# A two-layer hybrid decoder trunk: one near-bias row per head with zeros ahead of it, conditioning rows on VectorE alone, one of four branch scalings on ScalarE

## The chip, the cores and the metric

The kernel runs on one core of one Trainium2 chip. The metric is the device time of one execution in microseconds (us); less is better. The engines go by their profile names: PE is TensorE (matmuls and transposes), DVE is VectorE, ACT is ScalarE, POOL is GpSimd, SP is SyncE, which issues most of the transfers.

## What is computed

Two decoder layers on a sequence of 512 tokens of width 1024, batch 1, in float32. Each layer is a mixer and a SwiGLU feed-forward, both between norms that a conditioning vector c shifts, scales and gates:

```
for layer in range(2):
    shift, scale, gate = split(c @ mod_w[layer, 0] + mod_b[layer, 0], 3)
    h = rms_norm(x, norm_w[layer, 0, 0]) * (1 + scale) + shift
    y = mixer_ab(h) if layer == 0 else mixer_cd(h)
    x = x + gate * rms_norm(y, norm_w[layer, 0, 1])
    shift, scale, gate = split(c @ mod_w[layer, 1] + mod_b[layer, 1], 3)
    h = rms_norm(x, norm_w[layer, 1, 0]) * (1 + scale) + shift
    x = x + gate * rms_norm(swiglu(h), norm_w[layer, 1, 1])

# every softmax mixer, per head and block of 128 queries:
s = q @ k.T * scale + rel_tab[bucket(query - key)]     # masked where key > query
o = softmax(s) @ v
```

mixer_ab is native sparse attention (nsa: a compressed, a selected and a window branch, each times its own gate, 8 heads in 2 groups) beside sliding-window attention (swa). mixer_cd is block-sparse attention (moba) beside stick-breaking attention. The bias rel_tab depends on the distance of query and key alone, and is the same for all distances above some bound. With 512 tokens the selected branch of nsa takes all blocks and the window takes all keys, so both are plain causal attention with a bias, over other keys and values.

## The kernel before, in words

Matmuls of float32 data are made of three passes over operands split in a high and a low half: ACT writes the high half (L209), DVE the rest (L210), PE multiplies three times (L221 to L223). Weights stream through a ring of raw buffers that SP fills.

The program has one stage behind the other. In the profiled execution these are: the first norm and projections (to 75 us); swa attention, the compressed keys and the projections of keys and queries (75 to 162); nsa (162 to 245); the output projection of the mixer (248 to 302); the boundary to the first feed-forward (285 to 320); feed-forward 0 (to 670); the boundary and the projections of layer 1 (to 717); moba beside the value projections (717 to 800); stick-breaking (to 882); the output projection and feed-forward 1 (to 1300).

An **attention unit** is four heads of one group against one block of 128 queries, `qb` 0 to 3, so that it sees nk = 128, 256, 384 or 512 keys. `softmax_unit` (L619) makes, per head, two matmuls of the scores into PSUM (L631, L632), then on DVE a sum with the head's bias that also finds the row's minimum (one `tensor_tensor_reduce`, shown as CUSTOM_DVE_ANT; the minimum is fetched by a DVE_READ_ACCUMULATOR behind it), then the exponential on ACT (L646). `full` (L1011) takes the reciprocal of the sum and multiplies by the gate (L1020, L1022), scales the probabilities (`scale_p`, L680: one DVE instruction for all heads at L689 up to 256 keys; above that one per head, on ACT at L694 for as many heads as ACT_SCALE says, on DVE at L696 for the others), and multiplies by the values (`pv`, L650: transposes on PE at L659, a copy on ACT at L661, matmuls at L665). nsa has 16 such units (2 groups, 4 query blocks, selected and window branch), and the compressed branch is added by L1068 to L1073; its softmax is L1051 to L1062. moba has 8 units; there two of four heads were already scaled on ACT.

The bias is not zero only in the last 256 keys of a row. The **near table** NB (L344) holds a row of 256 zeros and, behind it, 256 biases per head; a head is a two-row view, zeros and its own row. A row with 512 keys is one instruction over this view (L637). A row with 384 keys is two: 128 keys with zeros (L641), then 256 with the biases, which starts from the minimum of the first (L644). A row with 256 or 128 keys is one (L644). The table is made twice: before nsa and before moba.

The **conditioning rows** (`mod_rows`, L352) are the product of c with columns of mod_w: a row of layer 0 is 8 steps over a 128x1024 tile of weights (SP loads it into a raw buffer, L377). A step is one DVE instruction that multiplies by a scalar per partition and adds to the sum (L384), or, for a row whose entry in ROW_DVE is 0, a scaling on ACT (L386) and an addition on POOL (L387). Rows 0 to 2 are stepped along with the query projections (two steps per projection) and the nsa units.

What is issued when is set by the scheduler of the language: each engine's instructions are put in an order by a timeline that it keeps for itself, so that every edit may move instructions near and far; each engine then runs its own list in that order and waits at its head. In nsa the front of a unit (scores to exponential) has priority over the back of the one before.

Of the kernel before, what the change touches and what calls it, by code (L numbers as in the profile page):

```python
# [10 lines left out]
F32 = mybir.dt.float32  # L11
F32R = mybir.dt.float32r
AF = mybir.ActivationFunctionType
ALU = mybir.AluOpType
# [115 lines left out]
class Trunk:  # L130
# [3 lines left out]
    MOD_ROW = 2  # L134
    ACT_SCALE = {"swa": 0, "nsa": 0, "moba": 2}
    AHEAD = {"swa": 0, "nsa": 60, "moba": 0}
    PIN = ("nsa",)
    ROW_DVE = (1, 0, 1)
    BIAS_AT = 4
# [204 lines left out]
    def near_table(self, pool):  # L344

        nb = pool.tile([P, 9, 256], F32, tag="NB", name=self.nm("NB"))
        self.nc.gpsimd.memset(nb[:, 0, :], 0.0)
        self.load_near(nb[:, 1:9, :], 0, 8)
        return [nb[:, 0:h + 2:h + 1, :] for h in range(8)]

# [268 lines left out]
    def softmax_unit(self, qb, heads, K, NB, init=None, far=True):  # L619
# [7 lines left out]
        for i, (q, nb) in enumerate(zip(heads, NB)):  # L627
# [6 lines left out]
            st = 3e38 if init is None else init[:, i:i + 1]  # L634
            two = lambda a: a.rearrange("p (b k) -> p b k", b=2)
            if nk == 512:
                red = nc.vector.tensor_tensor_reduce(two(pt), two(ps), nb[:, 0:2, :], 1.0, st, ALU.add, ALU.min, mx[:, i:i + 1])  # L637
            else:
                fw = max(nk - 256, 0)
                if fw:  # L640
                    nc.vector.tensor_tensor_reduce(pt[:, :fw], ps[:, :fw], nb[:, 0, :fw], 1.0, st,  # L641
                                                   ALU.add, ALU.min, mx[:, 4 + i:5 + i])
                    st = mx[:, 4 + i:5 + i]
                red = nc.vector.tensor_tensor_reduce(pt[:, fw:], ps[:, fw:], nb[:, nb.shape[1] - 1, 256 - (nk - fw):], 1.0,  # L644
                                                     st, ALU.add, ALU.min, mx[:, i:i + 1])
            nc.scalar.activation(pt, pt, AF.Exp, bias=mx[:, i:i + 1], scale=-1.0, accum_out=den[:, i:i + 1])  # L646
# [165 lines left out]
    def start(self):  # L812
# [26 lines left out]
        def feature(j):  # L839
            h = self.t_tmp("h", 2, 512)  # L840
            if j == self.BIAS_AT:
                self.bias_tables()
                self.skew_near(8)
                NBs = self.p_at.tile([P, 8, 256], F32, tag="NBs", name="NBs")
                self.load_near(NBs, 8, 8)
                self.NBs = [NBs[:, h:h + 1, :] for h in range(8)]
            acc = self.t_tmp("acc", 2, 256)
# [248 lines left out]
    def attention_ab(self):  # L1096
# [9 lines left out]
        self.skew_near(0)  # L1106
        self.NBn = self.near_table(self.p_at)
        
# [165 lines left out]
```

## Time and profile before

| what | value |
|---|---|
| median of 3 runs | 1304.86 us (1304.48 to 1305.43) |
| the profiled execution's own time | 1301.82 us |
| its span | 1300.0 us, 16642 instructions |
| granted TensorE clock, mean | 0.99 |
| PE busy | 1249.0 us, 96% |
| DVE busy | 683.3 us, 53% |
| ACT busy | 534.0 us, 41% |
| POOL busy | 92.2 us, 7% |

The shares are means over stages that differ much: in the feed-forwards PE is busy and DVE half idle, while in nsa DVE has hardly a gap. So the table says which engine carries the program as a whole, and the stage that an edit touches has to be read by itself. The profiled execution was 3.0 us under the median of the runs; the times in the trace count from the start of its span.

### The profile page before, as it was taken

How to read it: one execution, taken by the hardware profiler on the slowest of the kernel's cores; microseconds unless marked ns; L12 is line 12 of the kernel's file. 1: busy time of each engine (PE TensorE's matmuls, PEld its weight loads, DVE VectorE, ACT ScalarE, POOL GpSimd, SP SyncE). 2: the span in 40 equal slices, each digit the busy share in tenths (PEclk: the TensorE clock that was granted, in tenths of full speed). 3: DMA queues.
4: the chain of work that ended last, by engine and by line, in shares of the span. 5: the costliest groups of instructions: out<-in, count | busy, mean ns of one | idle time of the engine just before them, and what ended most of it. 6: DMA issues, size and time to landing. Idle time of an engine off the chain costs nothing.

```text
span 1300.0 us, 16642 instructions
## 1 busy us (share of the span) xinstructions
PE 1249.0 (96%) x6452; PEld 1021.2 (79%) x6452; DVE 683.3 (53%) x1158; ACT 534.0 (41%) x1015; POOL 92.2 (7%) x118
## 2 busy tenths in 40 slices
PE   6999999998999999999989999999999999999997
PEld 4887765687888888888879777878888888888885
DVE  6659799569457685342265555554733322224223
ACT  4447677642323223232242676773432222223221
POOL 1210600111000100000011000000000000000000
PEclk9999999998999999999999999999999999999999
DMA  9738602548547873333443113215433333333321
GB/s 382 248 91 259 195 21 95 199 145 338 209 152 264 330 259 98 97 96 97 127 162 103 49 50 86 61 34 210 178 85 104 96 96 96 96 97 96 96 97 65
DMA packets 52014, 183.88 MB, mean 141 GB/s; under 512 B 7185, under 2 KB 7329, under 8 KB 50912
## 3 DMA queue, kind: packets, MB, share of 16 engines
q1 hardware_dynamic: 46784, 171.57, 39.3%
q0 software_dynamic: 4720, 10.91, 3.1%
q8 instruction: 51, 0.84, 0.3%
q10 hardware_dynamic: 432, 0.35, 0.1%
q14 instruction: 27, 0.22, 0.0%
HBM read 170.11 MB, written 11.11 MB: 139 GB/s over the span
## 4 chain that ended last, share of the span: by engine, by line
PE 82%; DVE 8%; ACT 4%; DMA 3%; issue 3%; SPq 0%; POOL 0%; DVEq 0%; POOLq 0%; ACTq 0%
PE gu L222 12%; PE gu L223 12%; PE gu L221 12%; PE yacc L221 8%; PE yacc L223 7%; PE yacc L222 7%; PE mm L221 2%; PE mm L222 2%; PE mm L223 2%; PE oT L665 2%; PE z L1243 2%; PE PT L659 2%; DVE wlo L210 1%; PE S L631 1%; PE pc L221 1%
## 5 line engine op out<-in xcount | busy, mean ns | idle before, releaser
L210 DVE TENSOR_TENSOR wlo<-raw,whi 128x1024 fp32r<-128x1024 f32 (+1 forms) x182 | 218.3, 1205 | 372.1 <-ACT whi L209 371.3
L209 ACT ACTIVATE whi<-raw 128x1024 fp32r<-128x1024 f32 (+1 forms) x182 | 189.2, 1045 | 475.1 <-PE gu L222 274.0
L221 PE MATMUL gu<-act,whi 128*128 128x512 f32 (+1 forms) x768 | 284.7, 373 | 4.1 <-ACT act L495 4.1
L222 PE MATMUL gu<-act,whi 128*128 128x512 f32 (+1 forms) x768 | 286.3, 374 | 0.2 <-DVE act L496 0.2
L223 PE MATMUL gu<-act,wlo 128*128 128x512 f32 (+1 forms) x768 | 286.0, 373 | 0.0
L221 PE MATMUL yacc<-whi,act 128*128 128x512 f32 x480 | 186.4, 391 | 1.2 <-ACT whi L209 1.2
L222 PE MATMUL yacc<-wlo,act 128*128 128x512 f32 x480 | 186.7, 390 | 0.0
L223 PE MATMUL yacc<-whi,act 128*128 128x512 f32 x480 | 186.5, 389 | 0.0
L221 PEld LDWEIGHTS gu<-act,whi 128*128 128x128 f32 x768 | 145.0, 190 | 30.0 <-ACT act L495 5.0
L222 PEld LDWEIGHTS gu<-act,whi 128*128 128x128 f32 x768 | 145.9, 190 | 25.3 <-DVE act L496 0.4
L223 PEld LDWEIGHTS gu<-act,wlo 128*128 128x128 f32 x768 | 145.9, 190 | 24.9
L221 PEld LDWEIGHTS yacc<-whi,act 128*128 128x128 f32 x480 | 90.0, 188 | 21.0 <-ACT whi L209 1.7
L223 PEld LDWEIGHTS yacc<-whi,act 128*128 128x128 f32 x480 | 90.1, 188 | 18.8
L222 PEld LDWEIGHTS yacc<-wlo,act 128*128 128x128 f32 x480 | 90.1, 188 | 18.6
L384 DVE SCALAR_TENSOR_TENSOR macc<-act,col,macc 128x1024 f32<-128x1024 f32 x56 | 71.7, 1282 | 13.7 <-DMA macc<-in_mod_b 12.7
L646 ACT ACTIVATE act<-act,den 128x256 f32<-128x256 f32 (+3 forms) x128 | 68.2, 536 | 12.9 <-DVE den L644 9.5
L462 POOL TENSOR_TENSOR rms<-rms,col 128x1 f32<-128x1 f32 x32 | 25.2, 787 | 676.6 <-DVE rms L461 676.6
L221 PE MATMUL mm<-act,whi 128*128 128x512 f32 x160 | 64.2, 401 | 1.2 <-ACT NBc L338 1.2
L223 PE MATMUL mm<-act,wlo 128*128 128x512 f32 x160 | 63.1, 394 | 0.3 <-DVE wlo L210 0.3
L222 PE MATMUL mm<-act,whi 128*128 128x512 f32 x160 | 63.3, 395 | 0.0
L661 ACT ACTIVATE PT<-PT 128x512 f32<-128x512 f32 x74 | 41.4, 594 | 26.6 <-PE PT L659 26.4
L631 PE MATMUL S<-dup,stk 128*128 128x256 f32 (+3 forms) x128 | 44.2, 359 | 5.2 <-DVE den L644 2.7
(231 smaller groups left out, 1620.6 us busy)
## 6 DMA issues: line engine op xcount, KB each, us to landing
raw<-in_wfi SPq DMA_DIRECT2D x88, 512.0 KB, 3.6
act<-in_mod_w SPq DMA_DIRECT2D x28, 1024.0 KB, 7.2
raw<-in_wfo SPq DMA_DIRECT2D x44, 512.0 KB, 3.5
raw<-in_mod_w SPq DMA_DIRECT2D x24, 512.0 KB, 4.3
raw<-in_wcdf SPq DMA_DIRECT2D x18, 512.0 KB, 3.6
act<-in_mod SPq DMA_DIRECT2D x8, 1024.0 KB, 10.6
sc_x<-bnd SPq DMA_DIRECT2D x12, 512.0 KB, 2.7
bnd<-sc_x SPq DMA_DIRECT2D x12, 512.0 KB, 5.3
```

The lines of the kernel that those rows point to most:

```text
L209: nc.scalar.activation(hi[:, :n], raw[:, :n], AF.Copy)
L210: nc.vector.tensor_sub(lo[:, :n], raw[:, :n], hi[:, :n].bitcast(F32))
L221: nc.tensor.matmul(ps, a[0], b[0], start=start, stop=False)
L222: nc.tensor.matmul(ps, a[0], b[1], start=False, stop=False)
L223: nc.tensor.matmul(ps, a[1], b[0], start=False, stop=stop)
L384: nc.vector.scalar_tensor_tensor(accs[i], src, c, accs[i], op0=ALU.mult, op1=ALU.add)
L631: nc.tensor.matmul(ps, qs, K[:, 0, ks], start=True, stop=False)
L646: nc.scalar.activation(pt, pt, AF.Exp, bias=mx[:, i:i + 1], scale=-1.0, accum_out=den[:, i:i + 1])
L659: tr = nc.tensor.transpose(pp[:, m * P:m * P + P], Pt[:, i, c], self.ident)
L661: nc.scalar.activation(t, pp, AF.Copy)
L665: mm = nc.tensor.matmul(oT[DH * e:DH * e + DH, 0:256], V[:, kb], t[:, 256 * e:256 * e + 256], start=first and kb == lo_kb, stop=last and k ...
L1243: nc.tensor.matmul(z[i][:, a, l2:r], st, sph[k2 // 2][:, k2 % 2, 256 * p + l2:256 * p + r], start=False, stop=(k2 == nb - 1 and p == 1), s ...
```

## The change

Three edits in the program. The near table becomes one row of 512 per head, zeros in columns 0 to 255 and the biases behind them, so that a row of any number of keys is one instruction over the last nk columns; the zeros are written for 8 heads in place of one row, and the nsa table is taken from another pool of memory. Row 1 of the conditioning rows goes from ACT and POOL to DVE, as rows 0 and 2. In nsa the first of four heads of a unit with more than 256 keys is scaled on ACT, the other three on DVE; this holds for both the selected and the window branch, since both go through `scale_p`.

```
-    ACT_SCALE = {"swa": 0, "nsa": 0, "moba": 2}
+    ACT_SCALE = {"swa": 0, "nsa": 1, "moba": 2}
...
-    ROW_DVE = (1, 0, 1)
+    ROW_DVE = (1, 1, 1)
...
     def near_table(self, pool):
-        nb = pool.tile([P, 9, 256], F32, tag="NB", name=self.nm("NB"))
-        self.nc.gpsimd.memset(nb[:, 0, :], 0.0)
-        self.load_near(nb[:, 1:9, :], 0, 8)
-        return [nb[:, 0:h + 2:h + 1, :] for h in range(8)]
+        nb = pool.tile([P, 8, 512], F32, tag="NB", name=self.nm("NB"))
+        self.nc.gpsimd.memset(nb[:, :, 0:256], 0.0)
+        self.load_near(nb[:, :, 256:512], 0, 8)
+        return [nb[:, h, :] for h in range(8)]
...
-            two = lambda a: a.rearrange("p (b k) -> p b k", b=2)
-            if nk == 512:
-                red = nc.vector.tensor_tensor_reduce(two(pt), two(ps), nb[:, 0:2, :], 1.0, st, ALU.add, ALU.min, mx[:, i:i + 1])
-            else:
-                fw = max(nk - 256, 0)
-                if fw:
-                    nc.vector.tensor_tensor_reduce(pt[:, :fw], ps[:, :fw], nb[:, 0, :fw], 1.0, st,
-                                                   ALU.add, ALU.min, mx[:, 4 + i:5 + i])
-                    st = mx[:, 4 + i:5 + i]
-                red = nc.vector.tensor_tensor_reduce(pt[:, fw:], ps[:, fw:], nb[:, nb.shape[1] - 1, 256 - (nk - fw):], 1.0,
-                                                     st, ALU.add, ALU.min, mx[:, i:i + 1])
+            red = nc.vector.tensor_tensor_reduce(pt, ps, nb[:, nb.shape[1] - nk:], 1.0, st, ALU.add, ALU.min, mx[:, i:i + 1])
...
-                self.NBs = [NBs[:, h:h + 1, :] for h in range(8)]
+                self.NBs = [NBs[:, h, :] for h in range(8)]
...
         self.skew_near(0)
-        self.NBn = self.near_table(self.p_at)
+        self.NBn = self.near_table(self.p_tmp)
```

The scheduler then gives every engine another order in several places. Line numbers below are those of each kernel's own text; lines behind the near table's edit stand ten lines earlier in the changed kernel.

First place: DVE, at the end of swa and the first query projections, where rows 0 and 1 of the conditioning meet (macc is a row's sum, raw a weight tile, stk a query pair, act the probabilities). Before:

```order
L384 SCALAR_TENSOR_TENSOR macc_1387<-raw_1514,col,macc_1387 128x1024
L1003 RECIPROCAL fac_1058<-fac_1058 128x4
L1002 TENSOR_TENSOR fac_1085<-fac_1085,den_1037 128x4
L384 SCALAR_TENSOR_TENSOR macc_1387<-raw_1556,col,macc_1387 128x1024
L210 TENSOR_TENSOR wlo_1523<-raw_1520,whi_1522 128x1024
L689 TENSOR_TENSOR act_989<-act_989,fac_1058 128x4x256
L1003 RECIPROCAL fac_1085<-fac_1085 128x4
L250 SCALAR_TENSOR_TENSOR stk_1382<-mm_1357,stk_1382 64x512
L689 TENSOR_TENSOR act_989<-act_989,fac_1085 128x4x256
```

Now:

```order
L384 SCALAR_TENSOR_TENSOR macc_1387<-raw_1514,col,macc_1387 128x1024
L993 RECIPROCAL fac_1058<-fac_1058 128x4
L992 TENSOR_TENSOR fac_1085<-fac_1085,den_1037 128x4
L384 SCALAR_TENSOR_TENSOR macc_1517<-raw_1559,col,macc_1517 128x1024
L384 SCALAR_TENSOR_TENSOR macc_1387<-raw_1556,col,macc_1387 128x1024
L210 TENSOR_TENSOR wlo_1523<-raw_1520,whi_1522 128x1024
L679 TENSOR_TENSOR act_989<-act_989,fac_1058 128x4x256
L993 RECIPROCAL fac_1085<-fac_1085 128x4
L250 SCALAR_TENSOR_TENSOR stk_1382<-mm_1357,stk_1382 64x512
L384 SCALAR_TENSOR_TENSOR macc_1517<-raw_1670,col,macc_1517 128x1024
L679 TENSOR_TENSOR act_989<-act_989,fac_1085 128x4x256
```

The first step of row 1 (macc_1517, raw_1559) stands ahead of the last step of row 0, and its second ahead of the last swa scaling; the other six are spread over the query projections up to the compressed softmax.

Second place: ACT in nsa, group 0, the units with 384 and 512 keys (act with den is the exponential, PT the copy of transposed probabilities, sc the compressed branch). Before:

```order
L646 ACTIVATE act_1824,den_1823<-act_1824,den_1823 128x384 x2
L677 ACTIVATE act_1566<-oT_1703 128x2x128
L646 ACTIVATE act_1824,den_1823<-act_1824,den_1823 128x384 x2
L1056 ACTIVATE sc_1806<-sc_1806 128x512
L646 ACTIVATE act_1893,den_1892<-act_1893,den_1892 128x512 x4
L661 ACTIVATE PT_1870<-PT_1865 128x512
L661 ACTIVATE PT_1877<-PT_1872 128x512
L661 ACTIVATE PT_1884<-PT_1879 128x512
```

Now:

```order
L636 ACTIVATE act_1816,den_1815<-act_1816,den_1815 128x384 x3
L636 ACTIVATE act_1881,den_1880<-act_1881,den_1880 128x512
L667 ACTIVATE act_1566<-oT_1701 128x2x128
L636 ACTIVATE act_1881,den_1880<-act_1881,den_1880 128x512
L684 ACTIVATE act_1729<-act_1729,fac_1837 128x384
L1046 ACTIVATE sc_1798<-sc_1798 128x512
L636 ACTIVATE act_1881,den_1880<-act_1881,den_1880 128x512 x2
L651 ACTIVATE PT_1858<-PT_1853 128x512
L651 ACTIVATE PT_1865<-PT_1860 128x512
L651 ACTIVATE PT_1872<-PT_1867 128x512
```

The scaling of one unit's first head (L684) now stands between the exponentials of the next unit; eight such instructions come in nsa.

Third place: PE at the start of the mixer's output projection (yacc is the sum of one of three blocks of tokens, whi and wlo a weight tile's halves; each row occurs twice in the kernel, for two halves of the columns, and is given once). Before:

```order
L221 MATMUL yacc_2676<-whi_2604,act_1566 128x512
L222 MATMUL yacc_2676<-wlo_2605,act_1566 128x512
L223 MATMUL yacc_2676<-whi_2604,act_1567 128x512
L221 MATMUL yacc_2676<-whi_2610,act_1566 128x512
L221 MATMUL yacc_2741<-whi_2604,act_1566 128x512
L222 MATMUL yacc_2741<-wlo_2605,act_1566 128x512
L223 MATMUL yacc_2741<-whi_2604,act_1567 128x512
```

Now:

```order
L221 MATMUL yacc_2782<-whi_2580,act_1566 128x512
L222 MATMUL yacc_2782<-wlo_2581,act_1566 128x512
L223 MATMUL yacc_2782<-whi_2580,act_1567 128x512
L221 MATMUL yacc_2652<-whi_2586,act_1566 128x512
L221 MATMUL yacc_2717<-whi_2586,act_1566 128x512
L221 MATMUL yacc_2782<-whi_2586,act_1566 128x512
L222 MATMUL yacc_2652<-wlo_2587,act_1566 128x512
```

Before, six matmuls with the first weight tile (whi_2604) stood ahead of the first matmul with the second (whi_2610); now 18 with the first (whi_2580, all three blocks of tokens) stand ahead of the first with the second (whi_2586).

On POOL, the zeros and the load of the near table for moba stood ahead of the copies of the keys for moba (L268), and now stand behind the two of its first key tile. In nsa the table's zeros and load keep their place among POOL's transfers.

## Rows read from the trace of the kernel before

**Rows 1.** The page: engines' busy time and the chain that ended last, by engine.

```profile
PE 1249.0 (96%) x6452; PEld 1021.2 (79%) x6452; DVE 683.3 (53%) x1158; ACT 534.0 (41%) x1015; POOL 92.2 (7%) x118
...
PE 82%; DVE 8%; ACT 4%; DMA 3%; issue 3%; SPq 0%; POOL 0%; DVEq 0%; POOLq 0%; ACTq 0%
```

**Rows 2.** Windows: stretch, its length, busy us (instructions), clock, DMA share, GB/s.

```profile
core 0: us, PE busy (x) PEld busy (x) DVE busy (x) ACT busy (x) POOL busy (x), PEclk, DMA share, GB/s
140.00:150.00 10.00, 9.85 (x62) 7.15 (x61) 2.86 (x5) 8.54 (x12) 9.77 (x5) 1.00 0.52 160
...
172.00:217.00 45.00, 40.98 (x276) 25.99 (x276) 43.62 (x156) 32.70 (x99) 2.71 (x4) 1.00 0.26 76
217.00:245.00 28.00, 27.59 (x192) 16.26 (x191) 21.58 (x70) 22.26 (x53) 3.96 (x6) 1.00 0.17 53
...
717.00:800.00 83.00, 79.91 (x448) 62.77 (x447) 42.89 (x126) 57.98 (x130) 1.06 (x2) 1.00 0.19 58
```

**Rows 3.** The chain of waits in nsa: start, us on the chain, what.

```profile
174.37 0.40 DVE act L644
...
184.77 0.60 DVE act L637
...
187.05 1.53 PE PT L659 x12
...
216.74 1.06 PE PT L659 x8
```

**Rows 4.** Timeline of DVE: start, us, engine, line, operation, tiles, shapes.

```profile
173.45 0.28 DVE L641 CUSTOM_DVE_ANT_0 act<-S,NB 128x128 f32<-128x128 f32 x1
...
173.65 0.28 DVE L641 CUSTOM_DVE_ANT_0 act<-S,NB 128x128 f32<-128x128 f32 x1
```

**Rows 5.** Timeline of DVE: four scalings each (start to last end).

```profile
203.73 1.68 DVE L696 TENSOR_SCALAR act<-act,fac 128x512 f32<-128x512 f32 x4
...
223.96 1.41 DVE L696 TENSOR_SCALAR act<-act,fac 128x384 f32<-128x384 f32 x4
```

**Rows 6.** Line L694, moba's scalings on ACT: ns min/median/max, first to last.

```profile
L694 ACT ACTIVATE act<-act,fac x8: 598/670/727, 743.0 to 784.6; 128x384 f32<-128x384 f32 x4, 128x512 f32<-128x512 f32 x4
```

**Rows 7.** Groups by form, row 1's steps: busy, mean ns | idle before, releaser.

```profile
L386 ACT ACTIVATE raw<-raw,col 128x1024 f32<-128x1024 f32 x8 | 9.2, 1150 | 4.2 <-DMA raw<-in_mod_w 4.2
L387 POOL TENSOR_TENSOR macc<-macc,raw 128x1024 f32<-128x1024 f32 x8 | 21.2, 2646 | 4.0 <-ACT raw L386 3.6
```

**Rows 8.** Timeline of DVE where row 0 ends and POOL's additions of row 1 begin.

```profile
133.23 1.28 DVE L384 SCALAR_TENSOR_TENSOR macc<-raw,col,macc 128x1024 f32<-128x1024 f32 x1
...
135.80 1.22 DVE L689 TENSOR_TENSOR act<-act,fac 128x1024 f32<-128x1024 f32 x1
...
137.85 2.52 DVE L689 TENSOR_TENSOR act<-act,fac 128x1024 f32<-128x1024 f32 x1
```

**Rows 9.** Timelines of ACT (row 1's first step) and PE (nsa's first scores).

```profile
134.97 1.15 ACT L386 ACTIVATE raw<-raw,col 128x1024 f32<-128x1024 f32 x1 [0.35 <-DMA raw<-in_mod_w]
...
161.88 0.45 PE L631 MATMUL S<-dup,stk 128*128 128x128 f32 x1 [2.47 <-DVE stk L250]
```

**Rows 10.** Timeline at the start of the output projection, ACT and PE.

```profile
249.53 2.94 ACT L209 ACTIVATE whi<-raw 128x1024 fp32r<-128x1024 f32 x3
...
250.63 0.74 PE L221 MATMUL yacc<-whi,act 128*128 128x512 f32 x2 [1.25 <-ACT whi L209]
```

**Rows 11.** The chain of waits at the boundary to the first feed-forward.

```profile
290.50 8.19 DMA act<-in_mod_w
```

**Rows 12.** The near table for moba: POOL's timeline, its first use on DVE.

```profile
691.48 0.31 POOL L347 MEMSET NB<- 128x256 f32 x1 [1.43 <-DVE bnd L484]
...
709.63 0.52 POOL L268 DMA_DIRECT2D dup<-dup  x1 [0.80 <-DVE dup L267]
...
724.45 0.29 DVE L644 CUSTOM_DVE_ANT_0 act<-S,NB 128x128 f32<-128x128 f32 x1
```

**Rows 13.** The tile NB: its loads from issue to landing.

```profile
DMA to landing us min/median/max: 6.2/6.9/7.7
```

## The prediction

> **What bounds the kernel now.** Read the page first: PE is busy for 96% of the span and carries 82% of the chain that ended last, DVE 8% [rows 1]. An edit that takes work from DVE therefore pays only in stages in which DVE leads, and the second view, the windows by stage, says where that is [rows 2]. From 172 to 217 us, the first group of nsa and the start of the second, DVE is busy 43.62 of 45 us, PE 40.98, ACT 32.70. From 217 to 245 it is PE with 27.59 of 28, DVE 21.58. In moba, 717 to 800, PE has 79.91 of 83 and DVE 42.89. The third view, the chain of waits inside nsa, says the same in single steps [rows 3]: up to 216.74 it goes mostly through DVE (score sums), with one stretch of PE that begins at 187.05, and from 216.74 on through transposes and matmuls of PE. So the two edits that lighten DVE in nsa are worth something in about half of nsa, and nothing in the other half or in moba.
>
> **Edit 1, one instruction per score row.** Only rows with 384 keys change their count: 4 units in nsa, 16 rows, and 2 in moba, 8 rows. Such a row was an instruction over 128 keys, 173.45 to the next at 173.65, so 0.21 us with rounding [rows 4], and one over 256 at 0.40 [rows 3]: 0.61 together. The trace has no sum over 384. A row of 512 takes 0.60 [rows 3]; on the line between 128 and 512, 384 comes to 0.21 + 2/3 x 0.39 = 0.47. I take 0.47, so 0.14 saved per row; the bounds are 0.60 (as long as 512: 0.01 saved) and 0.40 (as 256: 0.21 saved). All 16 rows of nsa would give 2.2 us. The 8 of group 0 and about 4 of group 1 stand before 216.74: 12 x 0.14 = **1.7 us** on the path. The 8 rows of moba, 1.1 us, lie beside PE and count nothing; were PE not the cover, they would give those 1.1.
>
> **Edit 3, the first head of four on ACT.** Eight scalings leave DVE. Four of 512 took 1.68 us to their last end, four of 384 1.41 [rows 5]; with ends that overlap by some 0.1, that is 0.40 and 0.33 each. Group 0 has two of each: **1.5 us** off the path. Group 1's four, another 1.5, fall mostly behind 217, under PE: nothing. On ACT the same work costs 0.598 to 0.727 each by moba's rows [rows 6], some 2.6 us for group 0, and ACT has 12.3 us free in that window; the scaling stands between exponentials, and the work queued behind each is the next unit's exponentials, which transposes on PE wait for. I count that wait as hidden.
>
> **Edit 2, row 1 on DVE.** Removed: 8 scalings of 1.15 us on ACT and 8 additions of 2.65 us on POOL [rows 7]. Neither engine was on the chain there. Added: 8 instructions like row 0's, 1.28 us each [rows 8], 10.2 us on DVE between 133 and about 155. DVE's idle time there is 7.1 us in 140 to 150 alone [rows 2]. POOL's additions slowed DVE while they ran: the same scaling took 1.22 just ahead of them and 2.52 beside them [rows 8], so 1.3 us come back at the least. Against that the first of the new steps stands ahead of row 0's last step, at about 133.2, and its tile was there only when ACT could begin, at 134.97 less 0.1 [rows 9]: 1.7 us in which DVE's queue, with an operand split and the last swa scaling in it, stands still. The need is 10.2 + 1.7 - 1.3 = 10.6 us against 7.1 of idle time and shorter gaps on both sides. The first nsa scores (161.88, after DVE's last query copy, [rows 9]) come later by between 0 (the short gaps hold the rest) and 3.5. I take **1.0 later**, nearer the low end, because PE was busy 9.85 of 10 us in that window with projections that wait for little from DVE. The SP queue and the loads stay; the tiles come free earlier than with ACT and POOL behind each other, if anything.
>
> **Moves.** At the start of the output projection PE waited 1.25 us for the second weight tile's high half, behind three such copies on ACT [rows 10]. Now 18 instead of 6 matmuls of the first tile come ahead of that wait: 12 more, where two took 0.74 to the last end [rows 10], so some 3 to 4 us of work. I take **1.2 us gained**; the bounds are 0 (the copies come later by as much) and 1.25. At the boundary to the first feed-forward the chain goes through a load of conditioning weights for 8.19 us [rows 11]; the order of stores, loads and DVE steps is shuffled there. The price cannot be told from the order, since transfers share one path: I take 0, with 1.5 to either side, about a fifth of that wait. The near table for moba now starts behind the key copy, at 709.63 + 0.52. Its zeros are eight times as many as a write of 0.31: at most 2.5. The load takes 6.2 to 7.7 [rows 13], so it lands by 720.4, ahead of its first use at 724.45 [rows 12]: hidden, by 4 us. For nsa zeros and load keep their place on POOL, long ahead of the first use: nothing.
>
> **The sum.** -1.7 - 1.5 + 1.0 - 1.2 = -3.4 us. Against the profiled execution's own 1301.82 this is 1298.4. That execution stood 3.0 below the median of the runs, 1304.86; the same sum against the median gives **1301.5 us**. About 0.2%, 2.6 us, is what a measurement of this kernel can tell from no change.
>
> **Rivals.**
>
> *The gain in nsa is taken over by PE or ACT.* PE had only 4 us free of the 45 in DVE's window [rows 2], and half of its work there is short pieces that depend on ACT's copies; ACT gets 2.6 us more in its queue, ahead of exponentials that PE needs. Then edits 1 and 3 give nothing, and the sum is +1.0 - 1.2 = -0.2: 1304.7. For it speaks that PE already takes the lead at 187.05 within that window [rows 3]; against it that DVE's gaps in it are 1.4 us in all. [...] Chance of it all: 0.25.
>
> *A row of 384 costs as much as one of 512.* Then edit 1 saves 0.01 a row: the sum is -1.7, 1303.2. The even slope of 128, 256 and 512 speaks against it. Chance 0.05.
>
> *Slower: row 1 holds up DVE's queue.* The steps now wait for their tiles at the head of DVE's in-order queue, where the query copies, the compressed softmax and the swa scalings stand behind them. On ACT the same loads cost 4.2 us of waiting [rows 7]. With 10.2 + 4.2 - 1.3 = 13.1 us to place and only half of the 7.1 us usable, nsa starts 9.5 later, and the sum is -4.4 + 9.5 = +5.1: 1310.0. It decides from the point where the first scores of nsa start 7.0 later than 161.88, since 4.4 is gained elsewhere. Against it: the loads are issued by SP when a buffer comes free, and DVE alone frees it sooner than ACT did with POOL after it. [...] Chance 0.12.
>
> *Slower or even by moved transfers* (boundary, near table late in moba): +1.5 at the boundary with part of the gain lost, or the table landing behind 724.45. 1304 to 1308, chance 0.08, counted as slower.
>
> **How the numbers follow.** The forecast has 0.50, all of it faster by over 0.2%. The second case and the 384 rows make 0.30, within 0.2%. The last two make 0.20, slower. The low end takes every term at its best: -2.2 - 2.9 (both groups' scalings) - 1.25 - 1.5 at the boundary = -7.9, 1297.0. The high end reaches into the slower rival, to an nsa that starts about 8 us late: 1308.5. What is left out, about 0.2, is mostly the slower rival's upper half and gains outside these stages.
>
> **What the profile of the changed kernel would show.** Edit 1 right: sums over 384 at 0.45 to 0.50 start to start. Edit 3 right: eight scalings on ACT in nsa at 0.6 to 0.73, and a DVE window that is shorter by some 3 us, with the first output matmul that much earlier, net of the start. Edit 2 right: DVE's steps of row 1 with at most 2 us of waits for loads between 133 and 155, the scaling beside them at 1.2 and not 2.5, and the first scores of nsa at 162 to 164. The forecast is wrong if nsa's first scores come behind 166, if the wait of PE at the output projection comes back elsewhere, or if the length of nsa is unchanged while DVE's busy time in it falls.

## The result and the profile after

The changed kernel takes 1294.1 us (median of 6 runs, 1291.88 to 1295.78), the kernel before 1305.6 in the same comparison: a ratio of 0.990, 95% interval 0.9879 to 0.9921. It is faster, as forecast, but by 11.5 us and not by 3.4, and 3 us below the low end of the range (1297.0).

The page of the changed kernel, with its span, the busy times and the chain that ended last:

```profile
span 1293.7 us, 16573 instructions
...
PE 1246.0 (96%) x6452; PEld 1019.3 (79%) x6452; DVE 683.1 (53%) x1110; ACT 528.0 (41%) x1015; POOL 73.3 (6%) x110
...
PE 82%; DVE 7%; issue 5%; DMA 3%; ACT 3%; POOL 0%; SPq 0%; DVEq 0%; POOLq 0%; ACTq 0%
```

Against [rows 1] the shares hardly move; DVE has 48 instructions less and the same busy time (row 1's steps came, scalings and split sums went), and POOL lost 19 us. A page like this cannot say where 11 us went.

The page's group of the first pass of the output projections, with the idle time ahead of it in the last column:

```profile
L221 PE MATMUL yacc<-whi,act 128*128 128x512 f32 x480 | 186.0, 391 | 0.0
```

The groups by form of the sum over 384 keys and of the scalings on ACT (moba's eight and nsa's eight together):

```profile
L635 DVE CUSTOM_DVE_ANT_0 act<-S,NB 128x384 f32<-128x384 f32 x24 | 12.4, 550 | 2.4 <-PE S L632 2.4
...
L684 ACT ACTIVATE act<-act,fac 128x512 f32<-128x512 f32 x8 | 5.5, 714 | 0.2 <-DVE fac L1010 0.2
...
L684 ACT ACTIVATE act<-act,fac 128x384 f32<-128x384 f32 x8 | 4.7, 614 | 0.0
```

The wait of 1.25 us at the output projection [rows 10] is gone (0.0 idle ahead of L221 of yacc). The scalings cost what [rows 6] said.

DVE's timeline of the changed kernel, first row 1's first step with row 0's last and the two swa scalings behind it, then a score sum in nsa and the next one:

```profile
137.41 2.48 DVE L384 SCALAR_TENSOR_TENSOR macc<-raw,col,macc 128x1024 f32<-128x1024 f32 x2 [2.86 <-DMA raw<-in_mod_w]
...
140.94 1.22 DVE L679 TENSOR_TENSOR act<-act,fac 128x1024 f32<-128x1024 f32 x1
144.20 1.22 DVE L679 TENSOR_TENSOR act<-act,fac 128x1024 f32<-128x1024 f32 x1
...
178.34 0.55 DVE L635 CUSTOM_DVE_ANT_0 act<-S,NB 128x384 f32<-128x384 f32 x1
...
178.81 0.55 DVE L635 CUSTOM_DVE_ANT_0 act<-S,NB 128x384 f32<-128x384 f32 x1
```

A sum over 384 starts 0.47 us after the one ahead of it, as interpolated. DVE's queue stood 2.86 us for row 1's first tile (1.7 were forecast), and the swa scaling that took 2.52 beside POOL [rows 8] takes 1.22.

**Where the time went, by stage.** The stage lengths below are worked out from the starts of the first instruction of each stage in each trace: the first matmul behind the first projections (L318), the first score sum of nsa on DVE, the first output matmul, the 100th matmul after it, the 192nd matmul of the feed-forward after its first, the first projection of layer 1, the first moba scores, the first and the last stick-breaking matmul, the end. Two profiles each of the kernel before and of the changed kernel, unchanged; the second of each is among the runs below.

| stage (us) | before | before again | changed | changed again |
|---|---|---|---|---|
| first norm and projections | 75.3 | 76.2 | 76.4 | 76.3 |
| swa and the projections behind it, to nsa | 86.5 | 92.0 | 91.5 | 89.6 |
| nsa | 85.9 | 85.3 | 79.8 | 80.2 |
| start of the output projection | 24.4 | 23.8 | 22.8 | 22.8 |
| rest of it and boundary | 57.5 | 57.9 | 54.4 | 54.2 |
| feed-forward 0 | 346.1 | 346.1 | 346.1 | 345.6 |
| boundary and projections, to moba | 42.6 | 42.8 | 42.5 | 42.5 |
| moba | 70.2 | 71.8 | 69.7 | 69.7 |
| stick-breaking | 89.3 | 90.7 | 88.7 | 88.6 |
| to the end | 422.1 | 422.2 | 421.7 | 421.7 |
| span | 1300.0 | 1309.1 | 1293.7 | 1291.3 |

By the means of the two columns, nsa gave 5.6, the start of the output projection 1.3, the boundary 3.4, moba 1.3, stick-breaking 1.4, and the stretches ahead of nsa cost 1.9. The first profile of before had an unusually short way to nsa (86.5); every other kernel profiled has 88.1 or more there. So the profile that the forecast was made against was one of the fastest executions of this kernel: in the three later comparisons its 51 timed runs lie between 1300.99 and 1310.51, median 1307.2.

Part of these differences is the clock inside the stage. What a stage lost against full speed is (1 - clock) times its length. By this nsa lost 3.2 and 3.4 us in the two profiles of before, 0.0 and 1.7 in those of the changed kernel; the boundary 3.4 and 1.7 against none; moba and stick-breaking none in the first profile of before and 1.7 each in the second, against none; the two stretches ahead of nsa 0.2 and 3.4 against 3.4 and 1.7. The 3.2 of nsa lie in one window of the first profile (columns as in [rows 2]; the clock is the third number from the end):

```profile
160.00:170.00 10.00, 8.12 (x45) 7.27 (x45) 7.61 (x37) 7.22 (x29) 0.00 (x0) 0.66 0.13 46
```

So the 5.6 of nsa are not the two edits alone, and stages are best compared between profiles that lost alike.

### The profile page after: what moved, and what is told of

The parts are those of the page before. It is cut to its first block, busy times and chain, and to the rows that moved or that the text cites. A ratio compares the mean times of both kernels' runs of the same rounds, so it can differ in the third digit from the quotient of the medians.

```text
span 1293.7 us, 16573 instructions
## 1 busy us (share of the span) xinstructions
PE 1246.0 (96%) x6452; PEld 1019.3 (79%) x6452; DVE 683.1 (53%) x1110; ACT 528.0 (41%) x1015; POOL 73.3 (6%) x110
## 4 chain that ended last, share of the span: by engine, by line
PE 82%; DVE 7%; issue 5%; DMA 3%; ACT 3%; POOL 0%; SPq 0%; DVEq 0%; POOLq 0%; ACTq 0%
PE gu L222 12%; PE gu L223 12%; PE gu L221 12%; PE yacc L221 8%; PE yacc L223 8%; PE yacc L222 8%; PE mm L223 2%; PE mm L222 2%; PE mm L221 2%; PE oT L655 2%; PE PT L649 2%; DVE macc L384 2%; PE z L1233 2%; DVE act L635 1%; PE pc L221 1%
## 5 line engine op out<-in xcount | busy, mean ns | idle before, releaser
L221 PE MATMUL gu<-act,whi 128*128 128x512 f32 (+1 forms) x768 | 284.0, 372 | 4.4 <-ACT act L495 4.1
L221 PE MATMUL yacc<-whi,act 128*128 128x512 f32 x480 | 186.0, 391 | 0.0
L221 PEld LDWEIGHTS gu<-act,whi 128*128 128x128 f32 x768 | 144.0, 188 | 30.7 <-ACT act L495 5.0
L221 PEld LDWEIGHTS yacc<-whi,act 128*128 128x128 f32 x480 | 90.1, 188 | 19.4 <-issue 0.4
L384 DVE SCALAR_TENSOR_TENSOR macc<-act,col,macc 128x1024 f32<-128x1024 f32 x56 | 71.7, 1282 | 7.7 <-DMA macc<-in_mod_b 5.8
L221 PE MATMUL mm<-act,whi 128*128 128x512 f32 x160 | 65.1, 407 | 1.2 <-ACT NBc L338 1.2
L635 DVE CUSTOM_DVE_ANT_0 act<-S,NB 128x128 f32<-128x128 f32 (+3 forms) x96 | 43.1, 481 | 15.7 <-PE S L632 9.6
```

What stands on the lines that cost most here:

```text
L221: nc.tensor.matmul(ps, a[0], b[0], start=start, stop=False)
L384: nc.vector.scalar_tensor_tensor(accs[i], src, c, accs[i], op0=ALU.mult, op1=ALU.add)
L635: red = nc.vector.tensor_tensor_reduce(pt, ps, nb[:, nb.shape[1] - nk:], 1.0, st, ALU.add, ALU.min, mx[:, i:i + 1])
```

## What the runs differ in: the granted clock

These 51 runs of one program also differ in the mean granted clock of TensorE: at 0.992 they took 1302.3 on the average (2 runs), at 0.990 1304.3 (6), at 0.987 1308.7 (14). Time at the lower of the two levels (in windows of 1 us the first profile of before has 1.00 in 1269 of 1300, 0.50 in 22, and a mean between the two in 9) thus explains a good part of the spread, and of the gain. The loss is worked out as (1 - clock) times the span of a run, averaged over a kernel's runs; the last column is the mean time less this mean loss, and the ratio is always to the runs of the kernel before in the same comparison:

| kernel | runs | median us | ratio to before (95%) | clock | loss, us | time less loss, us |
|---|---|---|---|---|---|---|
| before | 51 | 1307.2 | | 0.985 to 0.992 | 15.7 | 1291.0 |
| changed | 6 | 1294.1 | 0.990 (0.9879 to 0.9921) | 0.992 to 0.993 | 9.5 | 1284.5 |
| changed, again | 5 | 1293.5 | 0.9899 (0.9883 to 0.9915) | 0.990 to 0.994 | 9.8 | 1284.2 |
| row 1 alone | 12 | 1301.9 | 0.9965 (0.9952 to 0.9978) | 0.988 to 0.993 | 13.3 | 1288.7 |
| near table alone | 5 | 1295.5 | 0.992 (0.9905 to 0.9935) | 0.991 to 0.993 | 10.1 | 1285.7 |
| ScalarE's scalings alone | 6 | 1297.6 | 0.9933 (0.9913 to 0.9954) | 0.987 to 0.994 | 11.2 | 1286.3 |
| near table and scalings | 5 | 1292.7 | 0.9893 (0.9877 to 0.991) | 0.993 to 0.994 | 8.5 | 1283.9 |
| the same, again | 4 | 1295.2 | 0.9906 (0.9891 to 0.9922) | 0.990 to 0.994 | 11.0 | 1284.1 |
| the same, two of four heads | 5 | 1299.4 | 0.9943 (0.9928 to 0.9957) | 0.987 to 0.989 | 15.3 | 1284.4 |
| one unit merged (third) | 12 | 1303.1 | 0.9981 (0.9966 to 0.9996) | 0.984 to 0.993 | 15.5 | 1288.6 |
| one unit merged (fourth) | 6 | 1301.8 | 0.9952 (0.9933 to 0.9971) | 0.989 to 0.993 | 13.0 | 1287.8 |
| moba's rows merged alone | 12 | 1305.1 | 0.9985 (0.9971 to 0.9999) | 0.984 to 0.991 | 15.6 | 1289.5 |
| near table, moba split | 6 | 1298.7 | 0.993 (0.9915 to 0.9944) | 0.990 to 0.993 | 11.2 | 1287.0 |

By the means some 12.7 us lie between before and changed: 6 are loss by the clock and 6.7 something else, if all of a loss were time. Not all of it is: within the kernel before a run with 1 us more loss is 0.7 us longer (a line through the 51 runs), so that the clock stands for some 4 to 6 us. PE also waits for other engines while its clock is low; a place at which a fall cost nothing is shown below.

**Where the clock falls.** In the kernel before, PE pauses at the boundary and in moba, and the clock is low for a few us behind some of the pauses. The windows of 10 us at the boundary of the first profile (length, PE, PEld, DVE, ACT, POOL busy, clock, DMA share, GB/s):

```profile
290.00:300.00 10.00, 7.69 (x39) 6.45 (x39) 8.48 (x12) 4.78 (x8) 2.00 (x2) 0.90 0.87 300
300.00:310.00 10.00, 9.84 (x77) 9.60 (x77) 9.56 (x12) 1.63 (x3) 1.45 (x1) 0.93 1.02 418
310.00:320.00 10.00, 7.96 (x52) 7.42 (x51) 9.78 (x11) 2.63 (x4) 0.35 (x1) 0.83 0.81 333
```

The same of the changed kernel:

```profile
290.00:300.00 10.00, 7.43 (x50) 6.27 (x48) 8.98 (x11) 2.70 (x6) 1.09 (x2) 1.00 0.99 381
300.00:310.00 10.00, 9.53 (x78) 9.29 (x78) 9.93 (x11) 1.94 (x5) 1.52 (x1) 1.00 1.03 420
310.00:320.00 10.00, 9.03 (x59) 8.00 (x60) 9.89 (x11) 2.51 (x5) 0.54 (x1) 1.00 0.66 238
```

And of the second profile of before, at the boundary, in moba and at the end of stick-breaking:

```profile
320.00:330.00 10.00, 9.15 (x53) 8.63 (x54) 9.89 (x10) 1.61 (x3) 0.54 (x1) 0.83 0.59 211
730.00:740.00 10.00, 9.23 (x44) 8.06 (x45) 6.37 (x22) 7.01 (x21) 0.00 (x0) 0.83 0.15 49
880.00:890.00 10.00, 9.60 (x60) 8.36 (x61) 3.23 (x10) 4.97 (x16) 0.00 (x0) 0.83 0.01 2
```

The falls come and go with the execution: in moba the first profile of before had none, the second had one, and the pause is the same. PE's timeline there, the first profile of before:

```profile
724.80 0.33 PE L631 MATMUL S<-dup,stk 128*128 128x128 f32 x1 [1.88 <-DVE den L644]
...
725.37 0.28 PE L631 MATMUL S<-dup,stk 128*128 128x256 f32 x1
```

and the second:

```profile
730.77 0.37 PE L631 MATMUL S<-dup,stk 128*128 128x128 f32 x1 [1.89 <-DVE den L644]
...
731.69 0.41 PE L631 MATMUL S<-dup,stk 128*128 128x256 f32 x1
```

After the same wait of 1.88 or 1.89 us for DVE, the same matmul takes 0.28 us in one and 0.41 in the other. The changed kernel has the wait too (1.88 us at 720.05) and no fall behind it in either of its profiles. Why the same pause has a fall behind it in one execution and none in another was not shown.

**The boundary itself.** Its length goes with the order of the queues and, at one place, with the clock. DVE's timeline in the kernel before, at the first tiles of the feed-forward:

```profile
293.38 0.69 DVE L496 TENSOR_TENSOR act<-tps,act 128x512 fp32r<-128x512 f32 x1
293.98 0.15 DVE L461 TENSOR_SCALAR rms<-rms 128x1 f32<-128x1 f32 x1
295.37 0.15 DVE L461 TENSOR_SCALAR rms<-rms 128x1 f32<-128x1 f32 x1 [1.25 <-ACT bnd L455]
295.44 1.28 DVE L484 SCALAR_TENSOR_TENSOR bnd<-bnd,rms,bnd 128x1024 f32<-128x1024 f32 x1
296.63 0.69 DVE L496 TENSOR_TENSOR act<-tps,act 128x512 fp32r<-128x512 f32 x1
```

and in the changed kernel:

```profile
291.65 1.28 DVE L484 SCALAR_TENSOR_TENSOR bnd<-bnd,rms,bnd 128x1024 f32<-128x1024 f32 x1
292.96 1.22 DVE L485 TENSOR_TENSOR bnd<-bnd,bnd 128x1024 f32<-128x1024 f32 x1
294.11 0.15 DVE L461 TENSOR_SCALAR rms<-rms 128x1 f32<-128x1 f32 x1
294.27 0.69 DVE L496 TENSOR_TENSOR act<-tps,act 128x512 fp32r<-128x512 f32 x1
```

Before, the operand split that PE needs (L496 at 296.63) stood behind a norm's step that waited 1.25 us for ACT and behind the product that follows it (L484). Now those come earlier, and the split starts at once. PE's timeline, before:

```profile
295.88 0.50 PE L221 MATMUL gu<-act,whi 128*128 128x256 f32 x2 [1.31 <-ACT act L495]
297.37 0.66 PE L492 MATMUL tps<-ident,bnd 128*128 128x128 f32 x4 [0.99 <-DVE act L496]
...
298.00 0.41 PE L223 MATMUL gu<-act,wlo 128*128 128x256 f32 x1
```

and now:

```profile
294.29 0.50 PE L221 MATMUL gu<-act,whi 128*128 128x256 f32 x2 [1.31 <-ACT act L495]
295.02 0.65 PE L492 MATMUL tps<-ident,bnd 128*128 128x128 f32 x4 [0.23 <-DVE act L496]
...
295.75 0.28 PE L221 MATMUL gu<-act,whi 128*128 128x256 f32 x1
```

Two waits close to each other (1.31 and 0.99) became 1.31 and 0.23. From the first matmul of the feed-forward to the 48th after it takes 9.8 and 10.1 us in the two profiles of before, 8.7 and 8.5 in those of the changed kernel. The matmuls behind the pair ran at the lower clock in the first profile of before (0.41) and at full clock in the changed kernel, but here the fall cost nothing: the second profile of before had none behind this pair and was no shorter. It ran ahead at full clock and waited longer (PE's gaps of more than 0.6 us in the whole stage, start to start, add up to 7.9 us against 5.6 in the first profile). At this place it is the order.

A second pair of waits stands some 18 us further on. DVE there, before and now:

```profile
312.75 0.69 DVE L496 TENSOR_TENSOR act<-tps,act 128x512 fp32r<-128x512 f32 x1 [0.18 <-ACT act L495]
313.35 1.27 DVE L384 SCALAR_TENSOR_TENSOR macc<-act,col,macc 128x1024 f32<-128x1024 f32 x1
314.54 0.69 DVE L496 TENSOR_TENSOR act<-tps,act 128x512 fp32r<-128x512 f32 x1
```

```profile
310.63 1.28 DVE L496 TENSOR_TENSOR act<-tps,act 128x512 fp32r<-128x512 f32 x2
```

A step of the conditioning rows (L384) stood between the two splits and now does not. PE, before:

```profile
313.25 0.73 PE L221 MATMUL gu<-act,whi 128*128 128x256 f32 x3 [0.74 <-ACT act L495]
315.29 1.11 PE L492 MATMUL tps<-ident,bnd 128*128 128x128 f32 x4 [1.30 <-DVE act L496]
...
316.41 0.41 PE L223 MATMUL gu<-act,wlo 128*128 128x256 f32 x1
```

the same place in the experiment "third unit" below, in which PE and the transfers have the order of before:

```profile
313.67 0.74 PE L221 MATMUL gu<-act,whi 128*128 128x256 f32 x3 [0.74 <-ACT act L495]
315.70 0.66 PE L492 MATMUL tps<-ident,bnd 128*128 128x128 f32 x4 [1.29 <-DVE act L496]
...
316.31 0.28 PE L223 MATMUL gu<-act,wlo 128*128 128x256 f32 x1
```

and the changed kernel:

```profile
310.56 0.51 PE L221 MATMUL gu<-act,whi 128*128 128x256 f32 x2 [0.74 <-ACT act L495]
311.37 0.49 PE L221 MATMUL gu<-act,whi 128*128 128x512 f32 x1 [0.31 <-DVE act L496]
```

The stretch from the 96th to the 144th matmul after the first holds this place. It takes 10.7 and 10.8 us in the two profiles of before, each with a fall behind the pair; 9.2 with the third unit, with the same two waits and no fall; 8.6 in both profiles of the changed kernel, with the second wait nearly gone and no fall. So here the fall costs 1.5 us and the order 0.6. Of the 3.4 us of the boundary some 1.9 are then the order (1.3 at the first pair, 0.6 at the second) and 1.5 the clock behind the second pair; the 9.2 rests on one profile.

## The experiments

Theory A is the forecast's own terms; theory B, formed on the trace of the changed kernel, says that most of the gain is the scheduler's order behind nsa and the clock. All kernels are made of the two in the study.

**The three edits one by one.** The near table's edit alone (the change without the lines of ROW_DVE and ACT_SCALE):

> The kernel before with the near table's edit alone (one score sum per row, zeros ahead of each head's biases); the conditioning rows and the scalings as before. Theory A (the forecast's terms): 12 rows of nsa on the path save 0.14 each, and the wait at the output projection goes: about 2.9 us under the kernel before, nothing at the boundary to the first feed-forward. Theory B (most of the gain is the order that the scheduler chose behind nsa, which is the same here as in the changed kernel): besides these also some 3 us between the first output matmul and the second column of the feed-forward, and some 1.2 in moba: 7 to 8 us under the kernel before.

Measured: 1295.5, ratio 0.992, which is 10.5 less where theory B had 7 to 8. nsa 82.9, start of the output projection 22.8, boundary 54.4, moba 69.7, stick-breaking 88.6. Theory B's places are right; with nsa 2.7 shorter than the mean of before this edit alone brings most of the change, though it takes only 24 sums away, each with the read of its minimum (DVE has 1110 instructions in place of 1158).

Row 1 alone:

```
-    ROW_DVE = (1, 0, 1)
+    ROW_DVE = (1, 1, 1)
```

> The kernel before with conditioning row 1 on VectorE alone. Theory A: nsa's first scores 1 us later (0 to 3.5), the time 1 us over the kernel before. Theory B, after the trace of the changed kernel: the first scores come 5 to 6 us later, since the queue of VectorE waits for a tile of conditioning weights; 2 us of it come back because the granted clock does not fall there; 2 to 4 us over the kernel before.

Measured: 1301.9, ratio 0.9965: 4.6 us faster, where both theories had it slower. Its way to nsa is 89.7, inside the 86.5 to 92.0 of the kernel before; the delay of 6 us that theory B read off was the first profile's short way to nsa, not the edit. The start of the output projection is 22.8 here too. Theory B fell on this point, and the slower rival of the prediction with it. Why the edit alone is faster is shown in part only: 2.4 us are less loss by the clock, 1.3 the start of the output projection; its boundary (57.4) is that of before, and its profile is of the slowest of its twelve runs, so that it does not show the rest.

ScalarE's scalings alone:

```
-    ACT_SCALE = {"swa": 0, "nsa": 0, "moba": 2}
+    ACT_SCALE = {"swa": 0, "nsa": 1, "moba": 2}
```

> The kernel before with the first of four heads scaled on ScalarE in nsa. Theory A: 1.5 us under the kernel before, all in nsa. Theory B: the same in nsa or less, and 1 to 3 us more at the boundary to the first feed-forward, where this kernel's transfers have the order of the changed kernel and VectorE nearly: 3 to 5 us under the kernel before.

Measured: 1297.6, ratio 0.9933, 8.7 less (interval 6 to 11). nsa 84.1 (1.5 less than the mean of before), boundary 53.4: the two places of theory B, and more than either number.

Near table and scalings without row 1 (the changed kernel with ROW_DVE back at (1, 0, 1)):

> The changed kernel with conditioning row 1 back on ScalarE and GpSimd. Behind nsa its order is that of the changed kernel. Theory A: 1 us faster than the changed kernel (0 to 3.5), by the earlier start of nsa. Theory B: nsa starts 5 to 6 us earlier than in the changed kernel, at a lower clock; 2 to 4 us faster than the changed kernel. If neither, and it is not faster, row 1 on VectorE brought something else.

Measured: 1292.7, 1.4 under the changed kernel; nsa 81.2, boundary 54.5. A second comparison ran both side by side:

> The changed kernel with row 1 back on ScalarE and GpSimd, a second time, in the same comparison as the changed kernel itself: 1 to 2 us faster than it, as between the two earlier comparisons (1292.7 and 1294.1).

> The changed kernel, unchanged, for a second profile and beside the run without row 1's edit. Theory B (fewer stretches at the lower clock are half of the gain): granted clock 0.992 to 0.994 again in every run, lower only before 75 us, near 140 to 160 and near 670; 1294 us. If the clock falls at 290 to 320, 720 or 870 as in the kernel before, its absence in the first profile was chance.

Measured: 1295.2 without row 1's edit, 1293.5 with it. The sign has turned, the intervals overlap, and the time less the loss differs by 0.1 to 0.6 us. On top of the other two edits row 1's is worth nothing that can be told, and no version here beats the changed kernel. The edits do not add: alone they bring 10.5, 8.7 and 4.6 us by their ratios, together 13; each of them alone already has the short start of the output projection (22.8), and two have the short boundary. The granted clock of the changed kernel was 0.992 to 0.994 in four runs and 0.990 in one. In its second profile it was lower near 130, 160, 670 and at the end, and not at the boundary or in moba.

**The kernel before a second time.**

> The kernel before, unchanged, for a second profile. Its timed runs (median 1307.2 us, mean granted clock 0.985 to 0.991) lie some 5 us over the profiled execution that the prediction was made against (1301.82, clock 0.990). Theory B: the difference is time at the lower clock, at the boundary to the first feed-forward (290 to 320 us) and in moba or at its end, where the profile of row 1 alone had it; the stretches between them are as long as in the first profile. Theory A has nothing to say on it; if the difference lies evenly over the span, theory B is wrong on this point.

Measured: span 1309.1, clock 0.986. The windows above show falls at 320, 730 and 880; another 5.5 us lie ahead of nsa, where PE fell to 0.66 in 130 to 140, which the expectation had not named. Nor had it named two falls in nsa (0.83 in 170 to 180 and in 200 to 210), where the first profile had one longer one; nsa is nearly as long in both (85.3 and 85.9).

**Order against work, with the same number of instructions.** The new near table, but only one nsa unit keeps one sum per row; all other units with 384 keys are split again. For the third such unit:

```
+        self.n384 = getattr(self, 'n384', 0) + (nk == 384)
...
+            if nk == 384 and self.n384 in (1, 2, 4, 5, 6):
+                nc.vector.tensor_tensor_reduce(pt[:, :128], ps[:, :128], nb[:, 128:256], 1.0, st,
+                                               ALU.add, ALU.min, mx[:, 4 + i:5 + i])
+                red = nc.vector.tensor_tensor_reduce(pt[:, 128:], ps[:, 128:], nb[:, 256:], 1.0,
+                                                     mx[:, 4 + i:5 + i], ALU.add, ALU.min, mx[:, i:i + 1])
```

> The new near table, but only the four rows of one nsa unit with 384 keys (group 1, selected branch) are one score sum; all other rows with 384 keys keep two. At the boundary to the first feed-forward transfers and PE have the order of the kernel before, VectorE all but two instructions. Theory A (work on VectorE decides): 0.3 us under the kernel before. Theory B (the order behind nsa decides): within 1.5 us of the kernel before.

Measured: 1303.1, ratio 0.9981, 2.5 less (interval 0.5 to 4.4): more than either theory's number, though the interval holds B's. Boundary 56.2, without a fall; the profile is of its fastest run. At the output projection PE has the order of before and yet no wait (23.0): the wait goes without the moved matmuls too.

For the fourth, the tuple is (1, 2, 3, 5, 6):

> As the run with the third unit, but the four rows are those of the next unit (group 1, window branch): the same number of instructions less. At the boundary transfers have the order of the changed kernel, and VectorE and ScalarE that of the kernel with ScalarE's scalings alone. Theory A: 0 to 0.3 us under the kernel before, since these rows lie under PE. Theory B: 5 to 8 us under the kernel before, and no stretch at the lower clock between 290 and 320 us.

Measured: 1301.8, ratio 0.9952, 6.3 less by the ratio. Boundary 54.6, as in the changed kernel, although the clock fell once there (0.83 in 310 to 320), which the expectation had excluded. Both kernels take away four sums with their reads (DVE has 1150 instructions in place of 1158); nsa is no shorter in the second (85.3 against 84.0); the boundary is 1.6 shorter, with the new order of its queues, although the fall costs 1.5 of it (10.1 us from the 96th to the 144th matmul; the kernels with nearly that order and no fall have 8.5 to 8.9). So at the boundary the order is worth over 1 us by itself, without DVE's work in nsa, by one profile of each. Over the whole run the two differ by 3.3 us in the mean, and 2.5 of that is loss by the clock.

**Moba's part.** One sum per row in moba alone (the split for stage nsa), and the opposite (the split for stage moba):

> The new near table with two score sums for 384 keys in nsa and one in moba (8 rows): nothing is lighter in nsa, and behind nsa the order is that of the kernel before up to moba. Theory A: moba's rows lie under PE, within 0.5 us of the kernel before. A third theory C (the rows of moba are on the path): 1 us under it or more. Theory B: within 1 us of the kernel before; what the changed kernel gains in moba is clock or order.

Measured: 1305.1, ratio 0.9985, 2.0 less; time less the loss 1.5 under before.

> The near table's edit alone, with moba's rows of 384 keys as two score sums again: what it has over the run of the near table alone is only moba (8 rows). At handover and boundary its order is that of the changed kernel. Theory A (moba lies under PE): the same as the near table alone, 1295.5 us, within 1. Theory C (the rows of moba are on the path, as the run that merged only those hints): 1.1 to 1.5 us over it. Theory D (moba's single sums also keep the clock up at 720 and 870 us): 3 to 5 us over it, with a mean granted clock of 0.990 or less and stretches at the lower clock at 720 or 870.

Measured: 1298.7, that is 3.2 over the near table alone by the medians and 2.5 by the means, 1.1 of it loss by the clock; by the ratios of the two comparisons it is 1.3, and their intervals overlap. The stages are clearer: moba 70.3 against 69.7, stick-breaking 89.3 against 88.6, with no fall in either. The two together take 159.5 or 159.6 us in the three profiles with two sums and no fall there (before, third unit, this one), and 158.3 or 158.4 in the five with one sum and no fall. Theory C holds: the eight rows of moba, with the order that goes with them, are worth 1.2 us by the stages and 1.3 to 1.5 by the time less the loss, though PE is busy for nearly all of it. Half of that shows only in the next stage. How, the chain of waits does not show: it names PE and little else in both. Theory D's time came, but not its sign: the clock was 0.990 to 0.993, and it did not fall at 720 or 870.

**More on ScalarE.** Two of four heads in nsa:

> As the last, with two of four heads scaled on ScalarE in nsa. If VectorE still leads in nsa's first part, another 1 to 1.5 us less; if ScalarE or PE has taken over, none, or up to 2.6 more. PE's order at the boundary is unchanged, VectorE's differs, so that a change behind 285 us is the order's.

Measured: 1299.4, some 5 over one head, where the expectation had at most 2.6. The windows of this kernel (columns as above):

```profile
196.00:208.00 12.00, 10.52 (x80) 7.52 (x81) 11.46 (x48) 12.00 (x40) 0.49 (x1) 1.00 0.38 108
...
230.00:240.00 10.00, 7.12 (x57) 4.59 (x55) 4.10 (x7) 8.49 (x18) 1.49 (x3) 0.88 0.49 151
...
720.00:730.00 10.00, 9.30 (x44) 8.04 (x45) 6.28 (x22) 7.05 (x21) 0.00 (x0) 0.83 0.17 51
870.00:880.00 10.00, 10.00 (x66) 8.81 (x66) 3.08 (x6) 5.26 (x12) 0.00 (x0) 0.87 0.15 48
```

ACT is now busy without a gap in 196 to 208, where DVE was with one head (12.00 of 12, ACT 10.85). nsa is 85.8 long, 4.4 more than with one head; it lost 5.1 by the clock, against 2.9 and 3.2. The clock falls near the end of nsa, in moba and in stick-breaking, where it did not with one head. The time less the loss is that of one head (1284.4 against 1284.0): in the runs the difference is as large as the loss by the clock. So a second head's scalings on ACT did not pay in nsa, while the first's did: nsa got 1.5 shorter with it alone.

## Why the prediction was wrong, step by step

- **Which stage each engine bounds: right in nsa, wrong in moba.** "The 8 rows of moba, 1.1 us, lie beside PE and count nothing": they counted 1.2 to 1.5 us, and the sentence had given 1.1 for the case that PE were no cover.
- **Edit 1 in nsa: right.** 1.7 was forecast on the path; with the near table alone nsa is 2.7 shorter than the mean of before (85.6). Part of that is the clock: this profile lost 1.7 us in nsa, those of before 3.2 and 3.4. Against row 1 alone, which has nsa's sums and scalings as before and lost the same 1.7 (nsa 84.8), it is 1.9 shorter. The price of a sum, 0.47, was exact.
- **Edit 3: right.** 1.5 forecast, 1.5 measured alone (84.1 against 85.6, with like losses of 3.4 and 3.3), and 1.6 on top of the near table (82.9 to 81.3). Both edits without row 1's, at like losses (2.9 and 3.2), have nsa at 81.2 and 81.5: 4.3 shorter, where 3.2 was forecast. The last 1.3 to the 80.0 of the changed kernel go with 2 us less loss.
- **Edit 2: wait seen, cost not.** The queue stood for 2.86 us in place of 1.7 (at most 2 was the sign), POOL's slowing of DVE went (1.22), and on top of the other two edits the time was the same with and without it. The 1.0 us of delay was not found. The row that the prediction takes for nsa's first scores, 161.88, is the first that waited for DVE; six stood ahead of it from 158.63 on. The same row starts at 168.07 in the changed kernel, behind the 166 that was to show the forecast wrong; but it does so at 168.37 in the second profile of before, so the sign could not tell.
- **The wait at the output projection: right,** 1.0 to 1.6 by stage, 1.2 forecast. The moved matmuls are not the only way to it, since with the third unit the wait went without them.
- **"The price cannot be told from the order ... I take 0, with 1.5 to either side" is the step that failed most:** the boundary gave 3.4, more than twice the bound. Some 1.9 of it are the order of DVE's queue, in which the split L496 no longer stands behind L484 and L384, and 1.5 the clock behind the second pair of waits. The waits of PE at 294 to 297 and 313 to 315 and the clock of 0.90, 0.93 and 0.83 could be read in the trace of before; that this order would shorten them was not worked out. The forecast looked at the transfers there, and in the trace of before a load does take longer there while others run: those of 1024 KB issued from 290.5 to 312.6 landed after 7.4 to 15.4 us, with the DMA share at 1.02 from 300 to 310, and the two issued at 320.6 and 323.2 after 4.9 and 5.0, with 0.72 from 320 to 326. But the waits that became shorter are PE's for DVE.
- **The base.** The sum was made against one profile at clock 0.990 and carried over to the median. The profile lay 5 us under the median of the later runs, and a term for time at the lower clock was missing altogether; that loss makes up to 6 of the 12.7 us between the two kernels. Which falls vanish with which order was not settled in general: in moba the same pause is followed by a fall in some executions and by none in others.
- **The slower rival** (row 1 holds up DVE's queue) named a wait that came, with a price that did not. The first rival (PE or ACT takes the gain over) did not come with one head on ACT, since nsa got shorter, and came with two.

So the direction came true by the steps that were forecast, in nsa and at the output projection, and the size did not: the boundary and moba's rows, put at nothing, gave 3.4 and 1.2 us, and the clock, which had no term, most of the rest. Why the clock fell less often in moba and stick-breaking behind the same wait stays open.

## What to carry to other kernels

A small edit under a scheduler changes the order everywhere behind it: compare the queues at the next place where several engines wait for each other, and price the pauses of PE there from the trace, as one would price an added instruction. Before costing anything, look at the mean clock of all runs beside the one that was profiled; if they differ by 0.3%, one profile is no base for terms of 1 us (here runs at 0.990 took 1304.3 us on the average and runs at 0.987 1308.7). And an experiment that removes the same few instructions in two places can tell work from order.

## What was not expected of the hardware

The same program ran between 1301.0 and 1310.5 us in 51 runs, with clocks of 0.992 to 0.985. A wait of PE of 1.88 us was followed by the lower clock in one execution and not in the next, with the same order of PE's queue there. The 24 steps of the conditioning rows held no surprise: 1.27 us each for 1024 columns in the changed kernel (1.28 were forecast), close to the 1.22 of a plain sum of two float32 sources (L485).
